# A feed-forward's first product as seven half-size products, on one core

## The chip, the core and the metric

The kernel runs on one core of one Trainium2 chip. The metric is the device time of one execution in microseconds. The engines are TensorE (PE in the rows, its weight loads PEld), VectorE (DVE), ScalarE (ACT), GpSimd (POOL), and SyncE (SP), which issues the transfers.

## What is computed

The reference is a transformer block of another kind followed by two layers of a second block, all on 512 tokens of 1024 features. What matters here is the feed-forward, which stands twice in each of the two layers, at the start and at the end:

```python
D_FF = 2816

def swiglu(x, w_in, w_out):
    g, u = jnp.split(x @ w_in, 2, axis=-1)
    return (jax.nn.silu(g) * u) @ w_out

for l in range(DEPTH_2):                                  # two layers
    x = x + 0.5 * swiglu(rms_norm_2(x, ffn1_norm[l]), ffn1_w_in[l], ffn1_w_out[l])
    ...                                                   # mixer, memory attention
    x = x + 0.5 * swiglu(rms_norm_2(x, ffn2_norm[l]), ffn2_w_in[l], ffn2_w_out[l])
    x = rms_norm_2(x, block_norm[l])
```

w_in is 1024 x 5632 (gate g, then up u), w_out is 2816 x 1024. All inputs are float32.

## The kernel before, in words

Activations stand transposed: features on the 128 partitions, the 512 tokens along the row. X(k), k = 0 to 7, are the eight 128 x 512 tiles of the residual stream.

**Three passes.** Every large product is made in a rounded type (float32r). Each operand a is split into its rounded value hi and the rest lo = a - hi, and TensorE adds hi*hi, hi*lo and lo*hi. `split` (line 367) does this for a tile: ScalarE rounds (371), VectorE subtracts (372), or 374 and 375 with a gain. `chunk3` (346) does it for weights: a transfer into a `raw` tile (358), ScalarE rounds into `wh` (361), VectorE subtracts into `wl` (362). `gemm_f` (377) issues the three matmuls for each contraction tile (383 to 385), each with its own load of 128 x 128 weights and 512 moving columns. `gemm_f2` (387) interleaves two such products at the start of a feed-forward, so that the last of the eight X tiles is needed late.

**Feed-forward.** `ffn` (1061) works in two halves of 11 inner features tiles each (a features tile is 128 of the 2816). For each one it brings in the weights of gate and up (128 x 2048 numbers, two transfers), makes gate in one PSUM bank and up in another (2 x 8 x 3 = 48 matmuls), multiplies by the norm's row R, applies Silu, multiplies (1076 to 1079) and splits the result into `hh`, `hl` (1080). After 11 tiles the second product runs: for each of the eight output tiles d, 11 x 3 matmuls, and VectorE adds half the sum to X(d) (1088). `Norm` (461) makes the feed-forward's input: for each k it splits gain * X(k) (eight ScalarE and eight VectorE operations of 512 columns), squares X(k) on ScalarE (483) and adds the squares up on GpSimd (488); the row R from these sums is needed only after the first product.

**Buffers.** Tiles come from pools with a fixed number of buffers: w 4 (each for `wh` and for `wl`, 1088 columns wide), x 4 and h 9 (128 x 4 x 512), b 9, p 5 and pt 4 (128 x 512), raw 2 (128 x 1088). PSUM has 3 banks acc, 2 ss, 3 st. The residual stream holds two of the nine h tiles.

**Order.** Each engine executes its own list strictly in order. The lists are written when the program is built: a planner takes the instructions in the order in which the code emits them, but lets a later one go ahead as soon as its inputs and buffers are ready in the planner's own model of time. So ScalarE rounds the next tile's weights before it finishes this tile.

**What the change touches.** The weights' layout in `prep` (line 208 on), `ffn`, and in `second_block` (1788) the places that make the feed-forward's input with `norm_split`. A new class `Blocks` stands beside `Norm`.

Of the kernel before, what the change touches and what calls it, by code (L numbers as in the profile page):

```python
# [18 lines left out]
L2 = 2  # L19
FF = 2816  # L20
NFF = FF // 128
HFF = NFF // 2
EPS = 1e-6
NEG = -1e30
CH = 2176
# [14 lines left out]
def _chunks(w, width):  # L40
    return np.stack([_ktile(w[:, i:i + width]) for i in range(0, w.shape[1], width)])


class Packer:
    def __init__(self):
        self.parts, self.at, self.n = [], {}, 0
# [82 lines left out]
def prep(I):  # L129
# [75 lines left out]

    for l in range(L2):
        for n in ("ffn1", "ffn2"):
            w = I[f"{n}_w_in_2"][l]
            w = np.concatenate([w[:, :FF].reshape(D, NFF, 128), w[:, FF:].reshape(D, NFF, 128)], axis=2).reshape(D, -1)
            A[f"{n}_a{l}"] = _chunks(w, 256)  # L210
            w = I[f"{n}_w_out_2"][l]
            A[f"{n}_b{l}"] = np.concatenate([_chunks(w[:FF // 2], 128), _chunks(w[FF // 2:], 128)])
        w = I["w_mix_in_2"][l]
        A[f"mixq{l}"] = _ktile(w[:, :256])
        A[f"mixkv{l}"] = _ktile(w[:, 256:384])
        sq = w[:, 416:672].reshape(D, 4, 64)[:, [0, 2, 1, 3]].reshape(D, 256)
        za = np.concatenate([w[:, 384:416], sq, w[:, 672:928]], axis=1)
        A[f"mixA{l}"] = _chunks(za, 272)
        A[f"mixN{l}"] = _chunks(w[:, 928:], 256)
        w = I["mla_w_uq_2"][l]  # L220
        A[f"uq{l}"] = np.stack([_ktile(w[:, :384]), _ktile(w[:, 384:])])
        A[f"ukv{l}"] = I["mla_w_ukv_2"][l].reshape(128, 2, 4, 2, 64).transpose(1, 0, 3, 2, 4).reshape(2, 128, 512)
        w = I["w_mix_out_2"][l]
        A[f"mixo_mla{l}"] = _chunks(w[:512], 256)
        A[f"mixo_swa{l}"] = _chunks(w[512:768], 512)
        A[f"mixo_na{l}"] = _chunks(w[768:], 512)
        A[f"memq{l}"] = _chunks(I["mem_w_q_2"][l], 256)
        A[f"memkv{l}"] = _chunks(I["mem_w_kv_2"][l], 256)
        A[f"memo{l}"] = _ktile(I["mem_w_o_2"][l])
        A[f"nab{l}"] = _bias_na(I["na_rel_bias_2"][l])  # L230
# [7 lines left out]
class Prog:  # L238
# [201 lines left out]
    def row(self, cols, R=None):  # L440
        ps = self.row_ps(cols)
        if R is None:
            R = self.p_r.tile([128, 512], F32, name="R", tag="R")
        self.nc.scalar.activation(R, ps, AF.Copy)
        return R
# [15 lines left out]
class Norm:  # L461
# [38 lines left out]
    def row(self):  # L500
        if self._R is None:
            self._R = self.g.row(self.cols())
        return self._R


def nat(i):
# [553 lines left out]

def ffn(g, name, l, xt, x, row, done=None):

    nc, A = g.nc, g.A
    X = tview(xt)
    wa, wb = A[f"{name}_a{l}"], A[f"{name}_b{l}"]
    for half in range(2):
        hh, hl = [g.h(F32R) for _ in range(3)], [g.h(F32R) for _ in range(3)]
        hv = [(hh[f // 4][:, f % 4], hl[f // 4][:, f % 4]) for f in range(HFF)]
        for f in range(HFF):
            wh, wl = g.chunk3(wa[half * HFF + f], 8)  # L1070
            pg, pu = g.acc(), g.ss()
            g.gemm_f2(pg, pu, wh, wl, 0, x) if half == 0 and f == 0 else (
                g.gemm_f(pg, wh, wl, 0, 128, x), g.gemm_f(pu, wh, wl, 128, 256, x))
            R = row()
            s, t = g.b(), g.b()
            nc.vector.tensor_tensor(s, pg, R, op=OP.mult)  # L1076
            nc.scalar.activation(s, s, AF.Silu)  # L1077
            nc.vector.tensor_tensor(t, pu, R, op=OP.mult)
            nc.vector.tensor_tensor(t, t, s, op=OP.mult)
            g.split(t, *hv[f])  # L1080
            g.tick()
        for d in range(KD):
            wh, wl = g.chunk3(wb[half * KD + d], HFF)
            cuts = (0, 256, T) if done and half and d == KD - 1 else (0, T)
            for c in map(slice, cuts, cuts[1:]):
                ps = g.ss()[:, c]
                g.gemm_f(ps, wh, wl, 0, 128, [(a[:, c], b[:, c]) for a, b in hv])
                nc.vector.scalar_tensor_tensor(X(d)[:, c], ps, 0.5, X(d)[:, c], op0=OP.mult, op1=OP.add)
                if done and half:
                    done(d, c)  # L1090
            g.tick()

# [695 lines left out]
def second_block(g, xt):  # L1788
# [1 line left out]
    X = tview(xt)  # L1790
    g.room(512, raw=2, k=1, p=5, pt=4)
    c2 = g.const("c2", g.at[2], g.p_k)
    norm = g.norm_split(X, g.c("ffn1_norm0"))
    x, row = norm.parts, norm.row
    for l in range(L2):
        ffn(g, "ffn1", l, xt, x, row)
        mem = mixer(g, l, xt, c2)
        memory(g, l, xt, mem)
        norm = g.norm_split(X, g.c(f"ffn2_norm{l}"))
        ffn(g, "ffn2", l, xt, norm.parts, norm.row, None if l + 1 < L2 else last_norm(g, xt, g.c(f"block_norm{l}")))  # L1800
        gb = g.c(f"block_norm{l}")
        if l + 1 < L2:

            gg = g.p_s.tile([128, 8], F32, name="gg", tag="gg", bufs=1)
            nc.vector.tensor_tensor(gg, gb, g.c(f"ffn1_norm{l + 1}"), op=OP.mult)
            norm = g.norm_split(X, gg)
            acc2 = None
            for k in range(KD):
                acc2 = norm.add(acc2, X(k), gb[:, k:k + 1])
            x, state = norm.parts, {}  # L1810

            def row(norm=norm, acc2=acc2, gb=gb, state=state):
                if not state:
# [34 lines left out]
```

## Time and profile before

| | |
|---|---|
| three runs | 2881.5, 2891.65 (median), 2895.55 us |
| the profiled execution | 2895.25 us, its span 2893.5 us |
| TensorE busy | 2827.5 us, 98% of the span |
| VectorE, ScalarE, GpSimd busy | 1458.4, 1162.8, 464.0 us |
| moved by DMA | 239.63 MB, 83 GB/s on the mean |

A profile shows one execution, instruction by instruction. A matmul's duration in it contains its way through the array, so that neighbours overlap; how fast they follow each other is read from their starts. The same holds, by less than 0.1 us, for other engines' operations. Where a row of the timeline has "x2", two neighbours of the same line were merged.

### The profile page before, as it was taken

How to read it: one execution, taken by the hardware profiler on the slowest of the kernel's cores; microseconds unless marked ns; L12 is line 12 of the kernel's file. 1: busy time of each engine (PE TensorE's matmuls, PEld its weight loads, DVE VectorE, ACT ScalarE, POOL GpSimd, SP SyncE). 2: the span in 40 equal slices, each digit the busy share in tenths (PEclk: the TensorE clock that was granted, in tenths of full speed). 3: DMA queues.
4: the chain of work that ended last, by engine and by line, in shares of the span. 5: the costliest groups of instructions: out<-in, count | busy, mean ns of one | idle time of the engine just before them, and what ended most of it. 6: DMA issues, size and time to landing. Idle time of an engine off the chain costs nothing.

```text
span 2893.5 us, 37993 instructions
## 1 busy us (share of the span) xinstructions
PE 2827.5 (98%) x15101; PEld 2399.4 (83%) x15101; DVE 1458.4 (50%) x2338; ACT 1162.8 (40%) x2008; POOL 464.0 (16%) x557
## 2 busy tenths in 40 slices
PE   8999999999999999999999999999999899999998
PEld 6798999888888888778888888888888778888887
DVE  5734455445434444677643444534444676644442
ACT  5323444533322235765432234322335765332232
POOL 4422222002000013512200003000013512200001
PEclk9999999999999999999799999999999999799999
DMA  4111222233323232212133323233232212133322
GB/s 154 52 45 59 74 73 74 73 103 122 99 87 105 86 106 75 68 37 66 38 102 90 107 88 108 88 85 112 84 107 70 63 40 72 31 102 90 107 88 80
DMA packets 78322, 239.63 MB, mean 83 GB/s; under 512 B 8512, under 2 KB 14656, under 8 KB 78016
## 3 DMA queue, kind: packets, MB, share of 16 engines
q1 hardware_dynamic: 78144, 237.20, 26.0%
q8 instruction: 119, 1.95, 0.3%
q14 instruction: 59, 0.48, 0.1%
HBM read 235.06 MB, written 2.10 MB: 82 GB/s over the span
## 4 chain that ended last, share of the span: by engine, by line
PE 91%; DVE 4%; ACT 2%; POOL 1%; issue 1%; DMA 0%; DVEq 0%; SPq 0%; ACTq 0%; POOLq 0%
PE ss L383 12%; PE ss L384 12%; PE ss L385 12%; PE acc L383 8%; PE acc L385 8%; PE acc L384 8%; PE acc L406 4%; PE acc L408 4%; PE acc L407 4%; PE st L413 3%; PE acc L1200 2%; PE ss L1236 2%; DVE b L611 1%; PE acc L396 1%; PE acc L395 1%; PE acc L397 1%
## 5 line engine op out<-in xcount | busy, mean ns | idle before, releaser
L362 DVE TENSOR_TENSOR wl<-raw,wh 128x1024 fp32r<-128x1024 f32 (+3 forms) x447 | 506.9, 1134 | 558.9 <-ACT wh L361 558.0
L361 ACT ACTIVATE wh<-raw 128x1024 fp32r<-128x1024 f32 (+3 forms) x459 | 449.9, 980 | 731.8 <-PE ss L384 533.7
L383 PE MATMUL acc<-x,wh 128*128 128x512 f32 x1048 | 412.7, 394 | 8.4 <-ACT wh L361 8.1
L385 PE MATMUL acc<-x,wl 128*128 128x512 f32 x1048 | 413.4, 394 | 0.1
L384 PE MATMUL acc<-x,wh 128*128 128x512 f32 x1048 | 411.3, 393 | 0.0
L383 PE MATMUL ss<-h,wh 128*128 128x512 f32 (+1 forms) x843 | 328.7, 390 | 0.0
L385 PE MATMUL ss<-h,wl 128*128 128x512 f32 (+1 forms) x843 | 326.1, 388 | 0.0
L384 PE MATMUL ss<-h,wh 128*128 128x512 f32 (+1 forms) x843 | 326.0, 388 | 0.0
L488 POOL TENSOR_TENSOR b<-b 128x512 f32<-128x512 f32 (+1 forms) x77 | 106.6, 1385 | 1176.6 <-ACT b L483 1068.6
L383 PE MATMUL ss<-x,wh 128*128 128x512 f32 x672 | 261.5, 389 | 0.1
L385 PE MATMUL ss<-x,wl 128*128 128x512 f32 x672 | 261.4, 389 | 0.0
L384 PE MATMUL ss<-x,wh 128*128 128x512 f32 x672 | 261.4, 389 | 0.0
L406 PE MATMUL acc<-wh,x 128*128 128x256 f32 (+1 forms) x880 | 252.8, 288 | 0.0
L407 PE MATMUL acc<-wl,x 128*128 128x256 f32 (+1 forms) x880 | 252.6, 288 | 0.0
L383 PEld LDWEIGHTS acc<-x,wh 128*128 128x128 f32 x1048 | 198.1, 189 | 50.8 <-ACT wh L361 8.5
L385 PEld LDWEIGHTS acc<-x,wl 128*128 128x128 f32 x1048 | 197.9, 189 | 42.6 <-DVE wl L362 1.6
L408 PE MATMUL acc<-wh,x 128*128 128x256 f32 (+1 forms) x816 | 232.1, 286 | 0.0
L384 PEld LDWEIGHTS acc<-x,wh 128*128 128x128 f32 x1048 | 197.9, 189 | 41.1 <-DVE x L375 0.6
L383 PEld LDWEIGHTS ss<-h,wh 128*128 128x128 f32 x843 | 159.3, 189 | 33.1 <-issue 0.6
L385 PEld LDWEIGHTS ss<-h,wl 128*128 128x128 f32 x843 | 159.5, 189 | 32.4
L384 PEld LDWEIGHTS ss<-h,wh 128*128 128x128 f32 x843 | 159.5, 189 | 31.6 <-issue 0.5
L1077 ACT ACTIVATE b<-b 128x512 f32<-128x512 f32 x88 | 55.6, 632 | 310.0 <-DVE b L1076 309.9
(384 smaller groups left out, 4813.6 us busy)
## 6 DMA issues: line engine op xcount, KB each, us to landing
raw<-in_ffn_a SPq DMA_DIRECT2D x176, 512.0 KB, 3.7
raw<-in_ffn_b SPq DMA_DIRECT2D x64, 384.0 KB, 3.1
raw<-in_ffn_b SPq DMA_DIRECT2D x64, 320.0 KB, 2.9
raw<-in_w_swa SPq DMA_DIRECT2D x36, 512.0 KB, 3.9
raw<-in_w_gate SPq DMA_DIRECT2D x16, 512.0 KB, 3.8
raw<-in_w_qkv SPq DMA_DIRECT2D x12, 512.0 KB, 3.9
raw<-in_mixN SPq DMA_DIRECT2D x12, 512.0 KB, 3.8
raw<-in_mixA SPq DMA_DIRECT2D x8, 544.0 KB, 3.7
```

Source lines behind the costliest of these rows:

```text
L361: nc.scalar.activation(h[:, s], r[:, s], AF.Copy)
L362: low.tensor_tensor(l[:, s], r[:, s], h[:, s].bitcast(F32), op=OP.subtract)
L383: mm(ps, a, xh, start=first and k == 0, stop=False)
L384: mm(ps, a, xl, start=False, stop=False)
L385: mm(ps, b, xh, start=False, stop=last and k == n - 1)
L406: mm(ps, a, wh[k][:, c0:c1], start=k == 0, stop=False, **part)
L407: mm(ps, a, wl[k][:, c0:c1], start=False, stop=False, **part)
L408: mm(ps, b, wh[k][:, c0:c1], start=False, stop=k == n - 1, **part)
L413: self.nc.tensor.transpose(ps[:, i * 128:(i + 1) * 128], src(i), self.ident)
L488: (engine or nc.gpsimd).tensor_tensor(acc, acc, sq, op=OP.add)
L1200: nc.tensor.matmul(self.pso[:, c:c + d], PT[:, hs(j * n + k)], self.v(lo + k, hj), start=k == 0, stop=k == n - 1)
L1236: nc.tensor.matmul(v3(s), self.q[h // 4][:96, i, hs(h % 4)], self.k[h // 4][:96, :, hs(h % 4)], start=True, stop=True)
```

## The change

For a features tile the two contraction halves (k 0 to 3, k 4 to 7), the two outputs (gate, up) and the two halves of the tokens (0 to 255, 256 to 511) make a 2 x 2 block product, which is done with seven products in place of eight (Winograd's variant of Strassen's form). `Blocks` makes the seven blocks of the input once per feed-forward, as sums of the two halves, each split into hi and lo; hi and lo of a block stand side by side in one 512-column row. For each features tile GpSimd makes the four sums of weight blocks. Each product has 4 contraction tiles and 3 passes of 256 columns, and its weights (128 x 512) are split one product at a time. The seven results are combined by accumulating in PSUM and by VectorE additions, with ScalarE copies of a bank between two of its products. The inner features are worked off in thirds of 6, 8 and 8 tiles in place of halves of 11. The next tile's first product is issued in the middle of this tile; loads come one tile ahead, into p tiles for even tiles and into raw tiles for odd ones.

```diff
-HFF = NFF // 2
+THIRDS = ((0, 6), (6, 14), (14, 22))
...
+class Blocks:
+    NAMES = ("11", "T1", "T3", "T2", "21", "22", "T4")
+    def __init__(self, g, xt, gain):
+        nc = g.nc
+        self.g, self.acc, self.n = g, None, T
+        self._rc = self._R = None
+        self.b = {n: g.x4() if i < 4 else g.h(F32R) for i, n in enumerate(self.NAMES)}
+        xs = {}
+        t1, t2 = slice(0, 256), slice(256, 512)
+        def put(name, j, src):
+            t = self.b[name]
+            g.split(src, t[:, j, t1], t[:, j, t2])
+        def diff(a, b):
+            d = g.b()[:, t1]
+            nc.vector.tensor_tensor(d, a, b, op=OP.subtract)
+            return d
+        T1 = g.h()
+        for k in range(KD):
+            x, j = g.b(), k % 4
+            nc.scalar.activation(x, xt(k), AF.Copy, scale=gain[:, k:k + 1])
+            if k < 4:
+                put("11", j, x[:, t1])
+                nc.vector.tensor_tensor(T1[:, j, t1], x[:, t2], x[:, t1], op=OP.subtract)
+                put("T1", j, T1[:, j, t1])
+                nc.gpsimd.tensor_copy(T1[:, j, t2], x[:, t2])
+            else:
+                put("21", j, x[:, t1])
+                put("22", j, x[:, t2])
+                d2 = diff(x[:, t2], T1[:, j, t1])
+                put("T2", j, d2)
+                put("T3", j, diff(x[:, t2], T1[:, j, t2]))
+                put("T4", j, diff(x[:, t1], d2))
+            self.acc = self.add(self.acc, xt(k), None)
+    add, cols, row = Norm.add, Norm.cols, Norm.row
...
 def ffn(g, name, l, xt, x, row, done=None):
...
+    def load(f):
+        if f % 2 == 0:
+            r = [g.p() for i in range(4)]
+        else:
+            r = [t[:, o:o + 512] for t in [g.p_raw.tile([128, CH // 2], F32, name="raw", tag="raw") for i in range(2)] for o in (0, 512)]
+        for i, t in enumerate(r):
+            nc.sync.dma_start(t, wa[f][:, i * 512:i * 512 + 512])
+        a11, a21, a12, a22 = r
+        S1, S2, S4 = (g.b() for i in range(3))
+        for d, a, b, op in ((S1, a21, a22, OP.add), (S2, S1, a11, OP.subtract), (a21, a11, a21, OP.subtract), (S4, a12, S2, OP.subtract)):
+            nc.gpsimd.tensor_tensor(d, a, b, op=op)
+        src[f] = dict(P1=a11, P2=a12, P3=S4, P4=a22, P5=S1, P6=S2, P7=a21)
+    def product(f, n, bank, first, xb):
+        if not slots:
+            h = g.p_w.tile([128, CH // 2], F32R, name="wh", tag="wh")
+            w = g.p_w.tile([128, CH // 2], F32R, name="wl", tag="wl")
+            slots.extend((h[:, o:o + 512], w[:, o:o + 512]) for o in (0, 512))
+        wh, wl = slots.pop(0)
+        g.split(src[f][n], wh, wl)
+        mm = nc.tensor.matmul
+        xt_ = x[xb]
+        for k in range(4):
+            a, b = wh[:, hs(k)], wl[:, hs(k)]
+            mm(bank, a, xt_[:, k, t1], start=first and k == 0, stop=False, skip_group_check=True)
+            mm(bank, a, xt_[:, k, t2], start=False, stop=False, skip_group_check=True)
+            mm(bank, b, xt_[:, k, t1], start=False, stop=k == 3, skip_group_check=True)
+    def keep(bank):
+        t = g.pt()[:, t1]
+        nc.scalar.activation(t, bank, AF.Copy)
+        return t
+    def begin(f):
+        ps[f] = g.acc()[:, t1]
+        product(f, "P1", ps[f], True, "11")
+        ps[f, "p1"] = keep(ps[f])
+    def tile(f, nxt, dst):
+        U, V, W = ps.pop(f), g.ss()[:, t1], g.st()[:, t1]
+        product(f, "P2", V, True, "21")
+        R = row()
+        s, t = g.b(), g.b()
+        nc.vector.tensor_tensor(s[:, t1], V, ps.pop((f, "p1")), op=OP.add)
+        nc.vector.tensor_tensor(s[:, t1], s[:, t1], R[:, t1], op=OP.mult)
+        product(f, "P6", U, False, "T2")
+        u2 = keep(U)
+        product(f, "P7", W, True, "T3")
+        product(f, "P5", U, False, "T1")
+        u4 = keep(U)
+        nc.vector.tensor_tensor(t[:, t2], W, u4, op=OP.add)
+        if nxt is not None:
+            begin(nxt)
+        product(f, "P3", U, False, "22")
+        nc.vector.tensor_tensor(s[:, t2], U, R[:, t2], op=OP.mult)
+        nc.scalar.activation(s, s, AF.Silu)
+        nc.gpsimd.tensor_tensor(s, s, R, op=OP.mult)
+        product(f, "P4", W, False, "T4")
+        nc.vector.tensor_tensor(t[:, t1], W, u2, op=OP.add)
+        nc.vector.tensor_tensor(t, t, s, op=OP.mult)
+        g.split(t, *dst)
+        src.pop(f)
+    load(0)
+    load(1)
+    begin(0)
+    for third, (f0, f1) in enumerate(THIRDS):
+        hh, hl = [g.h(F32R) for _ in range(2)], [g.h(F32R) for _ in range(2)]
+        hv = [(hh[f // 4][:, f % 4], hl[f // 4][:, f % 4]) for f in range(f1 - f0)]
+        for f in range(f0, f1):
+            if 1 < f + 1 < NFF:
+                load(f + 1)
+            tile(f, f + 1 if f + 1 < NFF else None, hv[f - f0])
             g.tick()
         for d in range(KD):
-            wh, wl = g.chunk3(wb[half * KD + d], HFF)
+            wh, wl = g.chunk3(A[f"{name}_b{l}{third}"][d], f1 - f0)
...
-    norm = g.norm_split(X, g.c("ffn1_norm0"))
-    x, row = norm.parts, norm.row
+    norm = Blocks(g, X, g.c("ffn1_norm0"))
+    x, row = norm.b, norm.row
```

The other places in `second_block` that made a feed-forward's input change in the same way, and `prep` stores the first product's weights by features tile in the order of the four blocks, and the second product's by thirds.

## Rows read from the trace of the kernel before

**Rows 1.** The page, parts 1 and 4: engines' busy time; the chain that ended last.
```profile
PE 2827.5 (98%) x15101; PEld 2399.4 (83%) x15101; DVE 1458.4 (50%) x2338; ACT 1162.8 (40%) x2008; POOL 464.0 (16%) x557
...
PE 91%; DVE 4%; ACT 2%; POOL 1%; issue 1%; DMA 0%; DVEq 0%; SPq 0%; ACTq 0%; POOLq 0%
```
**Rows 2.** Busy time by stretch, the first feed-forward: A:B, us long, engines (instructions).
```profile
735.00:1073.00 338.00, 338.00 (x1493) 279.85 (x1492) 148.71 (x182) 105.30 (x132) 8.25 (x6) 1.00 0.31 97
```
**Rows 3.** Timeline of PE, one features tile: start, duration, engine, line, operation, tiles.
```profile
1899.90 0.39 PE L383 MATMUL ss<-x,wh 128*128 128x512 f32 x1
...
1910.78 0.39 PE L383 MATMUL ss<-x,wh 128*128 128x512 f32 x1
```
**Rows 4.** Timeline of PE and of its weight loads, matmuls of 256 columns.
```profile
400.96 0.28 PE L406 MATMUL acc<-wh,x 128*128 128x256 f32 x1
...
403.84 0.28 PE L406 MATMUL acc<-wh,x 128*128 128x256 f32 x1
...
401.20 0.19 PEld L406 LDWEIGHTS acc<-wh,x 128*128 128x128 f32 x1
```
**Rows 5.** Timeline of DVE in a feed-forward; groups by line (count, busy us, mean ns).
```profile
743.31 0.68 DVE L1079 TENSOR_TENSOR b<-b 128x512 f32<-128x512 f32 x1
743.91 1.22 DVE L362 TENSOR_TENSOR wl<-raw,wh 128x1024 fp32r<-128x1024 f32 x1
...
L371 ACT ACTIVATE h<-b 128x512 fp32r<-128x512 f32 x88 | 55.7, 633 | 58.3 <-DVE b L1079 58.0
L1185 ACT ACTIVATE pt<-st 128x256 f32<-128x256 f32 x32 | 11.5, 382 | 14.9 <-PE st L413 14.9
```
**Rows 6.** Timeline of DVE and POOL where the second feed-forward's input is made.
```profile
1426.95 0.75 DVE L375 SCALAR_TENSOR_TENSOR x<-h,cst,x 128x512 fp32r<-128x512 f32 x1
1427.61 0.86 DVE L1735 TENSOR_TENSOR h<-h,acc 128x256 f32<-128x256 f32 x2
1428.39 1.84 DVE L375 SCALAR_TENSOR_TENSOR x<-h,cst,x 128x512 fp32r<-128x512 f32 x1
1430.16 0.41 DVE L1735 TENSOR_TENSOR h<-h,acc 128x256 f32<-128x256 f32 x1
1430.49 1.46 DVE L375 SCALAR_TENSOR_TENSOR x<-h,cst,x 128x512 fp32r<-128x512 f32 x1
...
1436.98 2.31 DVE L362 TENSOR_TENSOR wl<-raw,wh 128x1024 fp32r<-128x1024 f32 x1
1439.22 1.77 DVE L375 SCALAR_TENSOR_TENSOR x<-h,cst,x 128x512 fp32r<-128x512 f32 x1
1440.91 1.21 DVE L362 TENSOR_TENSOR wl<-raw,wh 128x1024 fp32r<-128x1024 f32 x1
...
1428.38 12.05 POOL L488 TENSOR_TENSOR b<-b 128x512 f32<-128x512 f32 x7 [40.50 <-issue]
```
**Rows 7.** Timeline of POOL and DVE where the other engine is not at work.
```profile
682.33 1.29 POOL L488 TENSOR_TENSOR b<-b 128x512 f32<-128x512 f32 x1 [8.94 <-ACT b L483]
...
715.08 0.74 DVE L375 SCALAR_TENSOR_TENSOR x<-h,cst,x 128x512 fp32r<-128x512 f32 x1
715.74 0.74 DVE L375 SCALAR_TENSOR_TENSOR x<-h,cst,x 128x512 fp32r<-128x512 f32 x1
```
**Rows 8.** Timeline of ACT and PE at that feed-forward's start: first, last and before it.
```profile
1425.87 0.72 ACT L374 ACTIVATE x<-h,cst 128x512 fp32r<-128x512 f32 x1 [1.87 <-DVE h L1735]
...
1436.34 0.62 ACT L483 ACTIVATE b<-h 128x512 f32<-128x512 f32 x1
...
1430.82 0.28 PE L385 MATMUL acc<-h,wl 128*128 128x256 f32 x1
```
**Rows 9.** Timeline of DVE: the last X before the first feed-forward of either layer.
```profile
712.75 1.28 DVE L1057 TENSOR_TENSOR h<-h,acc 128x512 f32<-128x512 f32 x2
...
1791.64 0.69 DVE L1088 SCALAR_TENSOR_TENSOR h<-ss,h 128x512 f32<-128x512 f32 x1 [1.26 <-PE ss L385]
```
**Rows 10.** The page, part 6: transfers of the first product's weights, KB each, us to landing.
```profile
raw<-in_ffn_a SPq DMA_DIRECT2D x176, 512.0 KB, 3.7
```

More of the change, by code (lines that the diff above doesn't have):

```diff
@@ L207, in prep @@
         for n in ("ffn1", "ffn2"):
-            w = I[f"{n}_w_in_2"][l]
-            w = np.concatenate([w[:, :FF].reshape(D, NFF, 128), w[:, FF:].reshape(D, NFF, 128)], axis=2).reshape(D, -1)
-            A[f"{n}_a{l}"] = _chunks(w, 256)
+            w = I[f"{n}_w_in_2"][l].reshape(2, 4, 128, 2, NFF, 128).transpose(4, 2, 0, 3, 1, 5)
+            A[f"{n}_a{l}"] = w.reshape(NFF, 128, 2048)
             w = I[f"{n}_w_out_2"][l]
-            A[f"{n}_b{l}"] = np.concatenate([_chunks(w[:FF // 2], 128), _chunks(w[FF // 2:], 128)])
+            for j, (a, b) in enumerate(THIRDS):
+                A[f"{n}_b{l}{j}"] = _chunks(w[a * 128:b * 128], 128)
         w = I["w_mix_in_2"][l]
@@ L1064, in ffn @@
     X = tview(xt)
[L1065 to L1080, printed above, removed]
+    wa = A[f"{name}_a{l}"]
@@ new lines, in ffn @@
+    t1, t2 = slice(0, 256), slice(256, 512)
+    src, slots, ps = {}, [], {}
+    def load(f):
[10 more added lines that the diff above has]
+        src[f] = dict(P1=a11, P2=a12, P3=S4, P4=a22, P5=S1, P6=S2, P7=a21)
@@ L1084, in ffn @@
-            cuts = (0, 256, T) if done and half and d == KD - 1 else (0, T)
+            wh, wl = g.chunk3(A[f"{name}_b{l}{third}"][d], f1 - f0)
+            last = done and third == 2
+            cuts = (0, 256, T) if last and d == KD - 1 else (0, T)
             for c in map(slice, cuts, cuts[1:]):
[L1086 to L1089, printed above, removed]
+                pd = g.ss()[:, c]
+                g.gemm_f(pd, wh, wl, 0, 128, [(a[:, c], b[:, c]) for a, b in hv])
+                nc.vector.scalar_tensor_tensor(X(d)[:, c], pd, 0.5, X(d)[:, c], op0=OP.mult, op1=OP.add)
+                if last:
@@ L1798, in second_block @@
         memory(g, l, xt, mem)
-        norm = g.norm_split(X, g.c(f"ffn2_norm{l}"))
-        ffn(g, "ffn2", l, xt, norm.parts, norm.row, None if l + 1 < L2 else last_norm(g, xt, g.c(f"block_norm{l}")))
+        norm = Blocks(g, X, g.c(f"ffn2_norm{l}"))
+        ffn(g, "ffn2", l, xt, norm.b, norm.row, None if l + 1 < L2 else last_norm(g, xt, g.c(f"block_norm{l}")))
         gb = g.c(f"block_norm{l}")
@@ L1805, in second_block @@
             nc.vector.tensor_tensor(gg, gb, g.c(f"ffn1_norm{l + 1}"), op=OP.mult)
-            norm = g.norm_split(X, gg)
+            norm = Blocks(g, X, gg)
             acc2 = None
@@ L1809, in second_block @@
                 acc2 = norm.add(acc2, X(k), gb[:, k:k + 1])
-            x, state = norm.parts, {}
+            x, state = norm.b, {}
             def row(norm=norm, acc2=acc2, gb=gb, state=state):
```

## The prediction

> **What bounds the kernel now.** The page's first part comes first: TensorE is busy 98% of the span, VectorE 50%, GpSimd 16%, and the chain that ended last runs through TensorE for 91% [rows 1]. Next, the stretch view of a feed-forward: in 338 us TensorE never rests and starts 1493 matmuls, 0.226 us each, while GpSimd works 8 us [rows 2]. So time there is matmuls times their spacing, and everything else hides. The timeline gives the spacing: 48 matmuls of 512 columns, one tile of the first product, start over 1899.90 to 1910.78: 10.88 us, 0.2267 each [rows 3]. (The 0.39 us beside each row is latency; only starts count.) Matmuls of 256 columns, which the change uses, run in the first block: 24 starts from 400.96 to 403.84, so 0.120 us each, though each loads its own weights for 0.19 us, so that these loads overlap [rows 4].
>
> **TensorE's own gain.** A tile of 128 features (there are 4 x 22 = 88) takes 7 products x 4 contraction tiles x 3 passes = 84 matmuls x 0.120 = 10.08 us in place of 10.88. Gain 0.80 us a tile, 70.4 us in all: not the eighth that the product count promises, since a narrow matmul costs more than half a wide one. The second product keeps its 528 wide matmuls per feed-forward. The Trainium skill (TensorE: Matmul & The Clock Gate, section Back-to-back issue gap) gives a lone spacing as columns over 2.4 GHz plus about 2.5 ns; worked out from that, an estimate is 48 x 0.216 - 84 x 0.109 = 1.2 us a tile, some 105 us in all, and the sum below would be 35 us lower. The rows stand 11 ns above that for either width, and they decide.
>
> **What the other engines now do per tile.** Before, VectorE and ScalarE were half idle. After, per tile:
> VectorE: seven low halves of weights, the product t*s and t's low half, nine 512-wide operations at 0.60 us start to start; five 256-wide ones at 0.33 [rows 5, 6]. That is 5.40 + 1.65 = 7.05 us of 10.08, if nobody disturbs it.
> ScalarE: seven roundings, Silu and t's rounding at 0.63, three copies out of PSUM at 0.38: 6.8 us [rows 5]. It hides.
> GpSimd: four sums of weights and s*R, each 1.29 us when alone [rows 7]: 6.5 us. It would hide too, but for VectorE.
>
> **GpSimd in VectorE's way.** The start of the second feed-forward is the one stretch where both work hard. Alone, a 512-wide VectorE operation there takes 0.74 us, 0.66 start to start [rows 7]. While GpSimd's seven sums run, it takes 1.46 to 1.84, and the 1024-wide one 2.31 in place of 1.22 [rows 5, 6]. The 256-wide additions L1735, which read one operand from PSUM, stay at 0.41 amid the same sums. So operations with both operands in SBUF wait for GpSimd, those with one in PSUM don't. From 1428.39 to 1440.91 VectorE did six of 0.66, one of 1.14 (1.22 less the 0.08 by which neighbours overlap) and three of 0.33: 6.1 us of work in 12.5, so that each of the seven sums cost it 0.92 us.
> A new tile has nine and a half such SBUF operations beside five of GpSimd. VectorE's cost is then 7.05 + 5 x 0.92 = 11.65 us, more than TensorE's 10.08 and the old 10.88. Bounds per GpSimd operation: 0 (it falls wholly into VectorE's rests) and 1.29 (VectorE waits for all of it); I take 0.92, the row whose mix of operations is nearest.
> The Trainium skill (SBUF — State Buffer, section Who interferes with whom) says that of two such operations the second is blocked until the first ends. The direction agrees with the rows; the size is less here, since operations with a PSUM operand get through.
>
> **What the slow tiles cost.** The excess shows only in runs of tiles: in a third's second product (8 features x 8 x 3 x 0.2267 = 43.5 us) TensorE needs little of VectorE, which gets ahead. How far is set by buffers: six weight slots beside the last chunk (3.6 us) and the four sums of one load (3.7 us); and the last tile's closing operations (1.5 us) lie under the second product. For 8 tiles: 93.2 - 8.8 = 84.4 against TensorE's 80.6, excess 3.8. The first third, 6 tiles, starts straight after the norm with three split products ahead: 69.9 - 1.8 - 3.7 - 1.5 = 62.9 against 60.5, excess 2.4. Per feed-forward 3.8 + 3.8 + 2.4 = 10.0, four times: 40 us. With 0 per GpSimd operation it is 0; with 1.29 (13.5 a tile) it is 17.1 + 17.1 + 12 = 46.2, four times 185.
>
> **The starts.** Before, TensorE runs into each feed-forward without a rest. Now Blocks gives VectorE 44 operations of 256 columns (3 for each of four k, 8 for each of the others) where the norm had 8, and ScalarE 28 roundings beside its 16 operations. P2 needs row block 21 of the last k, P6 and P7 sums from it.
> Second feed-forward of a layer: X is final only between 1425.87 and about 1433 [rows 6, 8]. VectorE from 1426.95: 44 x 0.33 = 14.5, six additions to X 2.0, seven sums of squares 6.4, four half-wide GpSimd copies about 1.8 by the same rate: 24.7, to 1451.7; block 21 of the last k seven operations earlier, 1449.4. TensorE's work before ends at 1431.1 [rows 8], P1 covers 1.4: idle 17. By ScalarE alone (19.8 us: 9.2 as now plus 28 x 0.38) it would be 11 to 12. I take 15, range 10 to 20, twice: 30.
> First feed-forward, layer 0: the last two X tiles land at 714.0 [rows 9]; 16 x 0.33 + 3 x 0.92, less the last seven: P2 at 719.8, TensorE idle from 712.8 but for P1: 5.6. Layer 1: one X tile late, at 1792.3 [rows 9]: about 2; there Blocks wants a tenth of nine h tiles, which waits for the old ones (up to 6 more). Sum 38, range 25 to 56.
>
> **Parts at nothing.** Copies of U between its products: ScalarE 0.38, behind one rounding 1.01; TensorE does another product meanwhile, 1.44 us. P4 waits for VectorE's t = W + copy, with P1 and P3 between (2.9 us). If a copy is late, all matmuls queued behind wait. Second product behind the last tile: the closing chain 0.33 + 0.60 + 0.63 + 0.60 + two GpSimd waits of 0.92 is 4.0 us; the other seven features cover 4.8, five cover 3.4 (before: ten, 6.8), so up to 0.6 once per feed-forward. SP issues four loads per tile for two; a load lands in about 3.7 us [rows 10] and has a tile's time. Third sums: 8 more additions to X per feed-forward, read from PSUM, in the idle stretch.
>
> **Sum** against the profiled execution, 2895.25 us (span 2893.5, 1.75 around it): -70.4 + 40 + 38 = +7.6, so 2902.9. That execution stands 3.6 above the median of the runs, so 2899.3: I say 2900. About 0.5% (14.5 us) is what a measurement of this kernel can tell from no change.
>
> **Rivals.**
> A, the forecast: VectorE held by GpSimd sets the tile's pace (11.4 to 12.0 us a tile, 21 to 68 us of excess, starts 30 to 40), 2871 to 2930. For it: rows 6. Chance 0.42.
> B: the two engines mesh. GpSimd works when VectorE waits or reads PSUM, the sums run in the second product, TensorE sets the pace: -70.4 + 0 + 30, so 2851 by the median. For it: a feed-forward's second products last 22 x 24 x 0.2267 = 120 us, in which GpSimd has nothing of its own to do; the per-tile work of either alone fits. Against: two tiles' buffers don't let sums go far ahead. 0.30.
> C, slower: the waits are longer and come on operations that hide nothing. Place: the runs of 8 tiles. Price by the worst of [rows 6], 2.31 - 1.22 = 1.09 per GpSimd operation: tile 12.5, excess 9.9 + 9.9 + 6.8 = 26.6 per feed-forward, 106 in all, starts 45: +81, so 2973. Gain and losses cancel at a tile of 11.55 us; from there each 0.1 us costs 7.8 in all. 0.19.
> D: VectorE waits for the whole of every GpSimd operation: -70.4 + 185 + 50, so 3056. 0.06. That would be the rule of the Trainium skill on blocking (SBUF — State Buffer, section Who interferes with whom) at its strictest.
> E, the gain isn't there: narrow matmuls with new weights each time run at the load's 0.19 us, 16.0 us a tile: +447, about 3340. Against: rows 4 show just this form at 0.120. 0.03.
> Faster by over 0.5% (under about 2877): most of B (0.27) and A's lower edge (0.04), 0.31. Within: 0.22 of A, 0.03 of B, 0.25. Slower: 0.16 of A, C, D, E, 0.44. The range, 2845 to 2985, holds A, nearly all of B and half of C. A's own is 2871 to 2930.
>
> **What would show it.** Matmuls of the first product 0.120 apart inside a product: the gain. GpSimd's 512-wide sums at 1.6 to 2.5 us, VectorE's 512-wide low halves at 1.2 to 1.8, VectorE busy near 100% in tiles of 11 to 12 us, TensorE waiting there for VectorE's wl: A or C. Tiles of 10.1 us with no wait: B. TensorE's longest rests at the two second feed-forwards' starts, 10 to 20 us, ended by VectorE or ScalarE. I am wrong if TensorE waits in the tiles for ScalarE or for loads, if tiles are even over a third, or if the starts cost nothing.

## The result and the profile after

| | before | after |
|---|---|---|
| median of the runs (four of either kernel) | 2889.73 us | 3118.03 us |
| lowest, highest | 2881.5, 2895.55 | 3110.38, 3123.47 |
| the profiled execution, its span | 2895.25, 2893.5 | 3123.47, 3121.6 |

The ratio is 1.079, 95% interval 1.0754 to 1.0826: 228 us slower, where 10 were forecast, and above the range of 2845 to 2985 us. The page of the changed kernel, parts 1 and 4, answers to [rows 1]:

```profile
PE 2850.6 (91%) x18260; PEld 2535.6 (81%) x18260; DVE 2053.3 (66%) x3186; ACT 1424.3 (46%) x2792; POOL 1168.2 (37%) x1013
...
PE 69%; DVE 19%; issue 6%; ACT 5%; POOL 1%; DMA 1%; DVEq 0%; SPq 0%; ACTq 0%; POOLq 0%
DVE wl L373 9%; PE ss L384 6%; PE ss L385 6%; PE ss L386 6%; PE acc L407 4%; PE acc L409 4%; PE acc L408 4%; PE acc L1145 3%; PE acc L1143 3%; PE acc L1144 3%; PE acc L384 3%; PE acc L385 3%; PE acc L386 3%; PE st L414 2%; DVE b L1163 2%
```

TensorE now rests 9% of the span, and a fifth of the chain lies on VectorE, half of that on the weights' low halves (wl, L373). The waits of the changed kernel (engine, tile and line waiting, releaser: us in total, times, longest) name the same pair:

```profile
POOL b L1129 <- DMA raw<-in_ffn_a: 336.5, 38, 27.2
...
ACT wh L372 <- PE acc L1144: 99.8, 58, 3.4
...
DVE b L1173 <- PE acc L1145: 65.6, 48, 3.0
...
PE ss L1145 <- DVE wl L373: 50.2, 60, 3.7
...
DVE b L1177 <- PE st L1145: 45.1, 47, 1.5
PE st L1145 <- DVE wl L373: 43.7, 27, 1.9
```

TensorE waits for low halves of weights, and VectorE waits for products (L1173, L1177). Neither of the two is the bound throughout. GpSimd's sums (L1129) wait most, for loads.

**Where the 228 us are.** A feed-forward is taken from the end of the VectorE addition that completes its X to the end of the one that completes the next. Before, the four last 360.5, 358.3, 364.1 and 363.5 us, after 416.8, 417.1, 418.1 and 421.4: 227.0 of the 228.1 by which the spans differ. Mixers and the first block are unchanged. TensorE's own work in one, 22 tiles and the second product's 528 matmuls, is 22 x 10.08 + 528 x 0.2267 = 341.5 us (before 359.1). So the four hold 307 us in which it rests or runs slowly, before 10.

**One pair of tiles.** The busy view of the changed kernel in two neighbouring stretches of the first feed-forward (A:B, us long, busy us and instructions of PE, PEld, DVE, ACT, POOL, granted clock, DMA share, GB/s):

```profile
879.18:891.24 12.06, 10.51 (x85) 9.98 (x83) 8.99 (x17) 5.70 (x11) 1.30 (x2) 1.00 0.39 120
891.24:905.85 14.61, 11.06 (x86) 10.45 (x86) 14.55 (x14) 6.28 (x14) 14.42 (x9) 1.00 0.21 67
```

and VectorE's and GpSimd's timelines inside the second (start, us, engine, line, operation, tiles):

```profile
896.42 1.52 DVE L1163 TENSOR_TENSOR b<-b,R 128x256 f32<-128x256 f32 x1
897.87 1.77 DVE L373 TENSOR_TENSOR wl<-raw,wh 128x512 fp32r<-128x512 f32 x1
899.56 1.77 DVE L373 TENSOR_TENSOR wl<-b,wh 128x512 fp32r<-128x512 f32 x1
901.26 0.41 DVE L1177 TENSOR_TENSOR b<-st,pt 128x256 f32<-128x256 f32 x1
```
```profile
897.62 1.47 POOL L1175 TENSOR_TENSOR b<-b,R 128x512 f32<-128x512 f32 x1
899.05 1.74 POOL L1129 TENSOR_TENSOR b<-p 128x512 f32<-128x512 f32 x1
900.86 1.59 POOL L1129 TENSOR_TENSOR b<-b,p 128x512 f32<-128x512 f32 x1
```

GpSimd makes eight sums and one s * R without a pause. In the lines above, VectorE's operations with two SBUF operands last 1.5 to 1.8 us, one for one with GpSimd's, while L1177, with an operand in PSUM, stays at 0.41. Of line 1163 (two SBUF operands), 34 rows lie wholly beside GpSimd's work: 31 of them last 1507 to 1524 ns and three 1066 to 1072, and the 47 beside none last 410 to 426. All rows of L1162, L1169, L1173 and L1177 (one operand in PSUM) last 406 to 425. This is what the Trainium skill states (SBUF — State Buffer, section Who interferes with whom): a VectorE instruction contends with a GpSimd instruction that reads SBUF if it has two SBUF inputs, and not if it has at most one and is outside VectorE's two-port modes. The trace agrees.
The slow stretch has 86 matmuls, 10.3 us of TensorE's work at 0.120 each, in 14.6 us. The quiet one has 85, 10.2 in 12.1, and VectorE is idle there for 3.1.

### The profile page after: what moved, and what is told of

It is laid out like the page before. It is cut to its first block, busy times and chain, and to the rows that moved or that the text cites. A ratio compares the mean times of both kernels' runs of the same rounds, so it can differ in the third digit from the quotient of the medians.

```text
span 3121.6 us, 47277 instructions
## 1 busy us (share of the span) xinstructions
PE 2850.6 (91%) x18260; PEld 2535.6 (81%) x18260; DVE 2053.3 (66%) x3186; ACT 1424.3 (46%) x2792; POOL 1168.2 (37%) x1013
## 4 chain that ended last, share of the span: by engine, by line
PE 69%; DVE 19%; issue 6%; ACT 5%; POOL 1%; DMA 1%; DVEq 0%; SPq 0%; ACTq 0%; POOLq 0%
DVE wl L373 9%; PE ss L384 6%; PE ss L385 6%; PE ss L386 6%; PE acc L407 4%; PE acc L409 4%; PE acc L408 4%; PE acc L1145 3%; PE acc L1143 3%; PE acc L1144 3%; PE acc L384 3%; PE acc L385 3%; PE acc L386 3%; PE st L414 2%; DVE b L1163 2%
## 5 line engine op out<-in xcount | busy, mean ns | idle before, releaser
L362 ACT ACTIVATE wh<-raw 128x1024 fp32r<-128x1024 f32 (+3 forms) x251 | 255.1, 1022 | 343.0 <-PE ss L385 116.7
L363 DVE TENSOR_TENSOR wl<-raw,wh 128x1024 fp32r<-128x1024 f32 (+3 forms) x239 | 281.7, 1185 | 180.7 <-ACT wh L362 180.1
L1145 PE MATMUL acc<-x,wl 128*128 128x256 f32 x1056 | 301.8, 292 | 38.9 <-DVE wl L373 38.5
L373 DVE TENSOR_TENSOR wl<-b,wh 128x512 fp32r<-128x512 f32 x264 | 293.6, 1114 | 56.5 <-ACT wh L372 56.0
L1143 PE MATMUL acc<-x,wh 128*128 128x256 f32 x1056 | 309.2, 293 | 12.9 <-ACT wh L372 11.4
L1144 PE MATMUL acc<-x,wh 128*128 128x256 f32 x1056 | 304.1, 289 | 8.3 <-DVE x L373 8.3
L1175 POOL TENSOR_TENSOR b<-b,R 128x512 f32<-128x512 f32 x88 | 129.8, 1475 | 412.9 <-ACT b L1174 412.9
L372 ACT ACTIVATE wh<-b 128x512 fp32r<-128x512 f32 x264 | 164.2, 624 | 237.2 <-PE acc L1144 85.4
L421 POOL TENSOR_TENSOR s<-s,half 128x4 f32<-128x4 f32 (+4 forms) x97 | 108.6, 1125 | 353.2 <-DVE s L420 341.8
L373 DVE TENSOR_TENSOR wl<-raw,wh 128x512 fp32r<-128x512 f32 x176 | 232.4, 1321 | 9.6 <-ACT wh L372 9.3
L384 PEld LDWEIGHTS ss<-h,wh 128*128 128x128 f32 x840 | 158.2, 189 | 55.8 <-ACT wh L362 13.6
L1129 POOL TENSOR_TENSOR b<-raw 128x512 f32<-128x512 f32 x44 | 61.5, 1397 | 339.2 <-DMA raw<-in_ffn_a 336.5
```

The source lines that it names most:

```text
L362: nc.scalar.activation(h[:, s], r[:, s], AF.Copy)
L363: low.tensor_tensor(l[:, s], r[:, s], h[:, s].bitcast(F32), op=OP.subtract)
L373: nc.vector.tensor_tensor(lo, src, hi.bitcast(F32), op=OP.subtract)
L384: mm(ps, a, xh, start=first and k == 0, stop=False)
L1143: mm(bank, a, xt_[:, k, t1], start=first and k == 0, stop=False, skip_group_check=True)
L1144: mm(bank, a, xt_[:, k, t2], start=False, stop=False, skip_group_check=True)
```

## The experiments

In all diffs the lines are of the changed kernel unless said otherwise. Each time is a median; ratios are to the kernel before on the same chip, with a 95% interval. The part of a profiled execution outside the four feed-forwards took 1435 to 1453 us from run to run, with no tie to the edit. Differences of some 15 us are therefore read from the feed-forwards' own sums (one execution each) and not from the medians.

**1. The sums on VectorE.**
```diff
-            nc.gpsimd.tensor_tensor(d, a, b, op=op)
+            nc.vector.tensor_tensor(d, a, b, op=op)
```


> The four weight sums of a tile go from GpSimd to VectorE; nothing else changes. Theory 1 (VectorE's operations on two SBUF operands alternate one for one with GpSimd's, and that slows the weight splits for which TensorE waits): VectorE has 7.05 + 4 x 0.60 = 9.45 us a tile and one GpSimd operation left to wait for, about 10.4 us a tile, so of the 57 us that a feed-forward's tiles lose now some 45 come back; 2900 to 2960 us. Theory 2 (the loads come late, because an odd tile's two raw buffers are given back late; who makes the sums is no matter): VectorE now waits for the load itself, with everything behind it; 3050 us or more.

2934.0 us, ratio 1.0153 (1.0067 to 1.0238). Theory 1, as forecast: 184 of the 228 us are back, although VectorE does 2.4 us more per tile by itself. Four tiles of this kernel, in the view by stretch:

```profile
857.18:898.50 41.32, 41.32 (x345) 41.23 (x344) 41.32 (x75) 23.97 (x48) 11.10 (x4) 1.00 0.34 104
```

Both engines are busy all the time, 10.3 us a tile: 7.05 + 2.4 + 0.92 for s * R is 10.37, the prediction's own prices. TensorE loses nothing beside a full VectorE: 345 matmuls at 0.120 are 41.4 us. Seven tiles in a row take 70.7 to 70.9 us in the second and last third of all four feed-forwards, where TensorE's own work is 70.6.

**2. No sums at all.** The products read loaded blocks (P3 a12, P5 a21, P6 a11); the sums are left out.

> The weight sums are left out: the products take plain weight blocks (a11, a21, a12) in place of S1, S2, S4 and the fourth sum. All loads, splits, matmuls and buffers stay. Theories 1 and 2 both: TensorE sets the tile's pace, 10.1 us a tile; what remains over TensorE's own work is the starts, 15 to 20 us each; 2860 to 2900 us. A third theory (the split of weights one product at a time, or the copies of a bank between its products, costs TensorE waits by itself): tiles of 11 us or more, over 2950 us.

2942.9 us, 1.0183 (1.0098 to 1.0269). Neither: what is left, some 53 us over the kernel before despite TensorE's 70 us gain, isn't the sums. It isn't VectorE's work either. Seven tiles take 73.7 or 76.3 us, more than with the sums on VectorE, though VectorE is busy for only 30.0 of 41.7 us in four tiles. The chain in 861 to 903 us holds no VectorE at all, but TensorE and ScalarE's roundings (wh), and these wait for products. The busy view of the four tiles, and this wait in 860 to 902:

```profile
859.60:901.30 41.70, 40.32 (x326) 39.20 (x325) 30.00 (x56) 22.70 (x47) 4.90 (x4) 1.00 0.33 102
```
```profile
ACT wh L372 <- PE acc L1141: 7.1, 4, 2.3
```

Number 18 comes back to this.

**3. Finer load buffers.** Four `raw` buffers of half the width in place of two, each load with its own.

> The same SBUF, but raw is four buffers of half the width in place of two, so that each of an odd tile's four blocks gives its buffer back by itself; every other user of raw loads in two pieces. Sums stay on GpSimd. Theory 2 or a mix of it with 1 (loads of odd tiles late, GpSimd idle before them and then eight sums in one run, VectorE at half pace during the run): the sums spread out, a pair of tiles falls from 26.1 us to 23 or 24, 2980 to 3040 us. Theory 1 alone (VectorE is full at 13 us a tile in whatever order the sums come): 3100 to 3130 us.

3125.9 us, 1.0817 (1.0718 to 1.0916). No change, as theory 1 alone has it. But GpSimd's 336 us of waiting for loads are still 301 here, so the edit hardly did what it was made for. That the loads aren't needed for the loss is shown by 13, where none of the first product's loads is waited for.

**4. The thirds alone**, in the kernel before.
```diff
-    for half in range(2):
+    for third, (f0, f1) in enumerate(THIRDS):
```


> The kernel before with one part of the change: the inner features in thirds of 6, 8 and 8 tiles. All theories: 8 more VectorE additions a feed-forward, hidden, and a shorter cover for the last tile of a third; 2885 to 2900 us. If thirds cost by themselves (TensorE waits at the third boundary of each feed-forward): 2900 to 2930 us.

2888.9 us, 1.0004 (0.9974 to 1.0034). Thirds cost nothing here.

**5. Sums made, not used.** The third sum goes into S1's buffer as well, so that a21 stays as loaded.
```diff
-        src[f] = dict(P1=a11, P2=a12, P3=S4, P4=a22, P5=S1, P6=S2, P7=a21)
+        src[f] = dict(P1=a11, P2=a12, P3=a12, P4=a22, P5=a21, P6=a11, P7=a21)
```


> The change, but the products read the loaded weight blocks themselves, as in the run without sums (2942.9 us), while GpSimd still makes four sums per tile, into buffers that nobody reads (the output differs). Theory 'contention': GpSimd's operations slow VectorE wherever they run, used or not; VectorE's work per tile is again 7.05 + 5 x 0.92 = 11.65 us, and the time goes back up to 3020 to 3120 us. Theory 'lateness': what costs is that products wait for sums that come late, not VectorE's pace; then the time stays near the run without sums, 2940 to 2980 us, though VectorE's 512-column operations still take 1.7 us beside a sum.

3197.0 us, 1.1075 (1.1025 to 1.1125): above even "contention". The theory that products wait for late sums falls. GpSimd's work, used by nobody, costs 254 us here.

**6, 7, 8. The starts.** In 6 to 8 the sums are on VectorE. 6: `R = row()` and its first use stand behind P3, the tile's sixth product. 7: also `put("22", ...)` and `put("T4", ...)` two steps later. 8: also `load(0)` and `begin(0)` in `Blocks`, ahead of k = 4.

> The sums on VectorE (2934.0 us by itself), and the norm's row R, with the multiplication of gate's first half by it, moved from behind the tile's second product to behind its sixth. In the trace of the run with sums on VectorE, TensorE's list holds the row's eight matmuls early in the first tile, and they wait for a GpSimd operation of 6.2 us (TensorE rests 729 to 732.9). Theory: that rest, 3.5 to 5.5 us at each of four starts, goes: 2910 to 2925 us. Rival: VectorE's work left over from the blocks is the end of that wait anyway, and the time stays at 2929 to 2939 us.

2918.0 us, 1.0113 (1.0067 to 1.0158). Inside the theory's range, but by luck, as the feed-forwards below show.

> As the run before this one, and in the making of the blocks the two that are used last (22 and T4) come two steps later, behind the blocks 21, T2 and T3 that the first products read. Theory 'order': TensorE rests at the starts because VectorE makes late blocks before early ones; 3 to 6 us less at each start, so 12 to 24 us below the run before this one. Rival 'amount': VectorE has some 12 us of work left when the last X tile is there, and TensorE waits for its end in any order: within 5 us of the run before this one.

2928.1 us, 1.0132 (1.0094 to 1.0171).

> As the run before this one, and the first tile's load, its four sums and its first product (which reads only blocks of the first four X tiles) are issued in the middle of the making of the blocks, in place of behind it. Theory: the sums and splits of the first tile's weights then stand ahead of the blocks of the last X tiles on VectorE, and some 5 us of the 12 us left over go; TensorE rests 5 us less at each start: 15 to 30 us below the run before this one, near or below the kernel before (2890 us). Rival: the blocks of the last tiles are then later by as much: within 8 us of it.

2922.8 us, 1.0125 (1.0096 to 1.0155). The row's wait that number 6 aims at stands in the timeline of experiment 1 (in brackets the idle time before, and what ended it):

```profile
732.90 2.07 PE L437 MATMUL ss<-cst,rc 128*128 128x128 f32 x8 [3.54 <-POOL rc L421]
```

It went, but the starts didn't shorten. From the completed X to the closing multiplication (t * s) of the third tile the four took 57.6, 64.2, 59.4 and 64.4 us in experiment 1 and 55.3, 67.2, 60.8 and 63.5 in 6; the sums of the four feed-forwards are 1479.7 and 1478.7, and the 15 us between the spans lie in the mixers, which the edit doesn't touch. So 6's theory falls, and 7's and 8's fall with it (1484.8 and 1482.8): neither row nor order is the limit.

**9. The sums spread out.** One sum behind each of P6, P7, the next tile's P1 and s * R; `sums` issues the next of the list.
```diff
-        for d, a, b, op in ((S1, a21, a22, OP.add), (S2, S1, a11, OP.subtract), (a21, a11, a21, OP.subtract), (S4, a12, S2, OP.subtract)):
-            nc.gpsimd.tensor_tensor(d, a, b, op=op)
+        todo.extend(((S1, a21, a22, OP.add), (S2, S1, a11, OP.subtract), (a21, a11, a21, OP.subtract), (S4, a12, S2, OP.subtract)))
...
+        sums(1)
```


> The change, with the same four sums per tile on GpSimd, but each issued behind another product of the tile (behind the sixth, the seventh, the next tile's first, and the fourth behind s * R), in place of all four ahead of the tile. In the trace of the change GpSimd makes eight sums and one s * R in one run of 14.6 us in every second tile, in which VectorE is at half its pace. Theory 'run': what costs is that run, because VectorE can get ahead by at most the eight product buffers; spread out, VectorE's average (11.65 us per tile) sets the pace in place of 13.0, and the time falls by some 88 x 1.35 = 119 us, to 2980 to 3050 us. Rival 'count': the number of GpSimd operations sets the cost wherever they stand: 3100 to 3135 us.

3113.5 us, 1.0798 (1.0724 to 1.0872): the range of "count". But the trace shows that the sums were hardly spread, since those of an odd tile still begin when its load lands (GpSimd's timeline):

```profile
884.53 1.30 POOL L1135 TENSOR_TENSOR b<-raw 128x512 f32<-128x512 f32 x1 [3.52 <-DMA raw<-in_ffn_a]
...
890.61 1.61 POOL L1183 TENSOR_TENSOR b<-b,R 128x512 f32<-128x512 f32 x1 [1.37 <-ACT b L1182]
...
896.30 1.61 POOL L1135 TENSOR_TENSOR b<-b,p 128x512 f32<-128x512 f32 x1 [0.68 <-POOL b L1135]
897.87 1.74 POOL L1135 TENSOR_TENSOR p<-p 128x512 f32<-128x512 f32 x1
```

Eight of GpSimd's operations stand in these 15.1 us, with 2.1 us of pauses. So this run doesn't decide between "run" and "count". That a run of eight isn't needed for the loss is shown by 13 (five in a row) and 14 (three).

**10. Half the sums.**
```diff
-            nc.gpsimd.tensor_tensor(d, a, b, op=op)
+            (nc.vector if f % 2 else nc.gpsimd).tensor_tensor(d, a, b, op=op)
```


> The change with the sums of the odd tiles on VectorE, so that GpSimd makes four sums and two s * R per two tiles. Theory 'amount': VectorE's work is 2 x 7.05 + 4 x 0.6 + 6 x 0.92 = 22.0 us per two tiles, 11.0 per tile against 10.1 with all sums on VectorE: 2934 + 88 x 0.9 = 3013, 2995 to 3040 us. Theory 'run': no run of eight sums is left, VectorE's lead covers four sums, and the tiles go back to 10.1 to 10.5 us: 2935 to 2975 us.

3071.8 us, 1.0658 (1.0583 to 1.0732). Above both. Half the sums keep 138 of the 184 us, with VectorE busy 45.0 of 50.3 us in four tiles:

```profile
873.56:923.82 50.26, 43.61 (x339) 42.20 (x338) 45.01 (x66) 23.79 (x48) 18.27 (x12) 0.97 0.28 85
```

So VectorE's mean doesn't set the time.

**11, 12. Squares on TensorE**: four one-column matmuls per X tile in place of GpSimd's additions, on 6 and on 8. The sums of squares, and so R, aren't the reference's in this form.

> As the run with the row later and all sums on VectorE (2918.0 us), and the sums of the norm's squares are added up by TensorE (four matmuls of one column per X tile, into one PSUM bank), in place of GpSimd's 8 additions at a start (16 at the third feed-forward, 12.2 us of GpSimd in one run there). Theory 'amount and port': VectorE's work left over at a start is slowed by these additions, up to 0.9 us for each that meets it; 3 to 8 us less at each start, 2888 to 2906 us. Rival: the small matmuls stand in TensorE's list and wait for ScalarE's squares, which gives as much back: 2912 to 2930 us.

2929.5 us, 1.0167 (1.0096 to 1.0237): the rival's range.

> As the run before this one, with the order of the run in which the first tile's load, sums and first product stand in the middle of the blocks (2922.8 us). Theory: the two add up, since with GpSimd out of the way the early sums run while VectorE has time: 2875 to 2898 us, within 0.5% of the kernel before or under it. Rival: the buffers that the early sums hold keep the blocks of the fifth and sixth X tile back, as in that run: within 8 us of the run before this one.

2920.2 us, 1.011 (1.0027 to 1.0193): neither. In 12 three starts shorten, to 54.1, 50.8 and 54.5, and the third lengthens to 71.0, because there TensorE works through the small matmuls of two rows, 64 in one run (its timeline in 12):

```profile
1821.67 11.55 PE L569 MATMUL st<-cst,b 128*128 128x1 f32 x64
```

**13, 14. GpSimd work without weights**, on experiment 2 (sums left out); 14 has `range(2)`.
```diff
+        z = g.b()
+        for i in range(4):
+            nc.gpsimd.tensor_tensor(z, z if i else R, R, op=OP.mult)
```


> The run without sums (2942.9 us), with four GpSimd multiplications per tile that read only the norm's row R and a buffer of their own, issued behind s * R: GpSimd is as busy as in the change, but waits for no load and keeps no weight buffer (the sums are left out, the output differs). Theory 'port': what costs is VectorE at half its pace beside GpSimd, and its lead of eight product buffers doesn't make that good: as the change or slower, 3090 to 3200 us. Theory 'average': the port costs only what brings VectorE over TensorE, 7.05 + 5 x 0.92 = 11.65 against 10.5 us per tile: 3020 to 3060 us, VectorE fully busy. Theory 'loop': in the change the sums delay the release of load buffers, and so the next loads; without that the port hurts little: 2943 to 2990 us.

3178.9 us, 1.0999 (1.096 to 1.1039): "port". Four GpSimd operations per tile that touch no load and no weight cost 236 us. "Loop" and "average" fall. Four tiles of it, and two of its waits (its line 1170 is the change's 1173, its 1142 the change's 1145):

```profile
878.86:930.71 51.85, 41.84 (x312) 39.38 (x311) 42.42 (x55) 22.35 (x46) 26.85 (x19) 0.97 0.26 78
```
```profile
DVE b L1170 <- PE acc L1142: 120.6, 76, 6.1
...
PE st L1142 <- DVE wl L373: 55.8, 51, 1.7
```

A tile lasts 13.0 us, with VectorE idle for 2.4 of it and TensorE not busy for 2.5: each waits for the other in turn.

> As the run before this one with two such multiplications in place of four. VectorE's work is 7.05 + 3 x 0.92 = 9.8 us per tile, under TensorE's 10.1. Theory 'port' (a run of slowed work isn't made good): about half of what four cost, 3010 to 3080 us. Theories 'average' and 'loop': no more than without them, 2935 to 2965 us.

2997.8 us, 1.0366 (1.0331 to 1.0402), between the two ranges. Two cost 55 us, four 236: a quarter, not half, but not nothing, although 7.05 + 3 x 0.92 = 9.8 is under TensorE's 10.08. Four tiles:

```profile
861.03:903.41 42.38, 39.84 (x312) 37.81 (x311) 34.41 (x55) 22.26 (x46) 14.11 (x11) 1.00 0.30 94
```

One rival to the port would be that the planner wrote other lists when GpSimd got more to do. The traces exclude it: by lines and tile names, VectorE, ScalarE and TensorE execute the same operations in the same order in 14 as in 2. In 13 only six or seven of VectorE's operations, two of ScalarE's and a handful of TensorE's stand a few places elsewhere in each feed-forward. What differs is GpSimd's work and the time that VectorE's operations take beside it. The chain shows where that falls: VectorE isn't on it in four tiles of 2, and in 14 its low halves (L373, wl) hold 12% of it and the closing t * s (L1178) 6%, in 13 20% and 9%.

**15. No differences in Blocks.**
```diff
-                put("T3", j, diff(x[:, t2], T1[:, j, t2]))
+                put("T3", j, x[:, t2])
```
and likewise T2 and T4.

> As the run with the row later and all sums on VectorE (2918.0 us), with the blocks T2, T3 and T4 split from the scaled X itself: 12 of the blocks' 44 VectorE operations per start, 4.5 us at 0.375, are left out (the output differs). Theory 'amount': TensorE waits at a start for VectorE's work left over, and each microsecond less of it is worth one or more, since TensorE runs at half its clock behind the rest: 4 to 8 us per start, 2886 to 2902 us. Rival: what is waited for at the starts is ScalarE, buffers or loads: 2908 to 2924 us.

2907.3 us, 1.0061 (1.0039 to 1.0082). 10.7 us less by the medians, between the two. The feed-forwards' sums fall by 16.7 (1478.6 to 1461.9): 12 VectorE operations of 4.5 us in all are worth some 4 us per start. So VectorE's amount counts there, nearly one for one, at the lower edge of "amount".

**16. The version that the runs then pointed to.**

> All sums on VectorE, the row later, the first tile's load, sums and first product amid the blocks; the squares of the first, second and fourth feed-forward added up by TensorE into 32 columns of a PSUM bank (VectorE adds the eight of each), those of the third, which needs two rows, on GpSimd as in the change but each beside its own X tile and not all at the end. In the run with both rows' squares on TensorE the first, second and fourth start took 54.1, 50.8 and 54.5 us against 55.3, 67.2 and 63.5 with the row later alone, and the third 71.0 against 60.8. Theory: the third goes back to 60 and the others stay: 2920 - 11 = 2909, 2895 to 2915 us, still slower than the kernel before. Rival: it gets under 2890 us, if the third gains as the others do.

2914.3 us, 1.0091 (1.0058 to 1.0124), as forecast. The starts sum to 217 us against 247 in 6, but the next three tiles of the second and fourth feed-forward give 15 of the 30 back. It is still slower than the kernel before.

**17, 18. Half the lead**, on 13 and on 2.
```diff
-            slots.extend((h[:, o:o + 512], w[:, o:o + 512]) for o in (0, 512))
+            slots.append((h[:, :512], w[:, :512]))
```


> The run with four GpSimd multiplications per tile that touch no weights (3178.9 us), with one product's weights in each of the four weight buffers in place of two, so that VectorE can be at most four products ahead of TensorE in place of eight. Theory 'lead': a tile costs more than either engine's mean because VectorE, slowed for some 8 us and free for some 5, can't work ahead far enough; with half the lead more of the slowed stretch falls on TensorE: 3210 to 3330 us. Rival: the lead has no part in it: 3160 to 3200 us.

3140.6 us, 1.0921 (1.0848 to 1.0994).

> The same halving of the buffers in the run without sums and without those multiplications (2942.9 us). There VectorE has 3 us to spare in each tile and is slowed by s * R alone, so both theories expect little: 2940 to 2975 us. A larger rise would say that four buffers are too few by themselves, and the run beside this one would tell nothing.

2896.6 us, 1.0044 (1.0011 to 1.0078). Both are below all that was expected. By the medians they are 38 and 46 us faster than 13 and 2, by the feed-forwards' sums 33 and 37, so the theory of the short lead falls; the price of the four operations, 244 us between these two, is that of the longer lead (236). In 18 seven tiles take 71.5 to 72.7 us, so most of what number 2 lost in its tiles is gone. A reason that fits the waits in 2 is that a buffer with two products' weights comes free only when both are used. It isn't shown alone, since the planner wrote other lists for 17 and 18. Single buffers together with real sums on VectorE weren't tried.

## Why the prediction was wrong

The account from the feed-forwards' sums: -70.4 from TensorE's work, +103.7 for what remains with the sums on VectorE (1479.7 less 4 x 341.5 is 113.7, before 10.0), +193.7 for the sums on GpSimd (1673.4 - 1479.7); together 227.0. Forecast: -70.4, +38, +40. The 103.7 lie at the starts, since the later tiles of experiment 1 take no longer than TensorE's own work. Of the 193.7, some 24 lie there as well: up to the third tile's t * s the four feed-forwards take 270 us in the change and 246 in experiment 1.

**TensorE's gain: right.** Of 7392 matmuls of the first product 6717 follow their neighbour by 0.10 to 0.14 us.

**VectorE's price: right.** 7.05 + 5 x 0.92 = 11.65 us per tile makes 46.6 in four; a stretch of four tiles in the second third of the changed kernel shows 46.68 busy, in 54.37 us:

```profile
879.18:933.55 54.37, 44.37 (x338) 42.37 (x336) 46.68 (x57) 23.98 (x48) 31.45 (x20) 0.97 0.27 78
```

**"What the slow tiles cost": wrong, and this is the step that failed.** It took the tile's time as VectorE's work, 11.65 us, and credited 8.8 us per run of eight tiles for VectorE getting ahead. A tile took 12.2 to 13.3 us (85.2 to 93.0 over seven). Eight tiles, with TensorE's time in the second product taken off, took 95 to 105 us where the sum had 84.4, so the credit was not there either. Tiles even over a third were one of the prediction's own signs of being wrong. Charged 40 us, it cost 194, some 170 of them behind the starts. Experiments 13 and 14 show in its place that GpSimd at work beside VectorE makes the tile longer than either engine's own work, even at 9.8 us of VectorE's work. A full VectorE alone doesn't do that: in experiment 1 both engines are busy all the time and nothing is lost. Why VectorE's idle time couldn't be used is not settled. Loads that come late (13), lateness of the sums (5), other lists (14) and a short lead (17) are excluded as its cause, and a run of eight isn't needed (13, 14). The clock is a part: in the change some 400 of the first product's matmuls run at the lower clock, about 40 us over 0.120 each, in experiment 1 140, about 14 us. What is left for the rest is the fixed order of the lists, in which a slowed operation holds back those behind it: in 13 VectorE stands 121 us before L1170 waiting for a product, and TensorE behind for a low half that comes later in VectorE's list. That is argued from the waits and wasn't tried.

**The starts: right in place, too small by more than half.** Charged 38 us, they cost about 104 with the sums on VectorE. The first feed-forwards of the two layers, charged 5.6 and 2, lost 21 and 20; the second ones, charged 15 each, 31 and 32. Nor was it one rest of 10 to 20 us: TensorE's longest at a start of the changed kernel is 6.3. The bounds given with the 38, 25 and 56, don't follow from its terms, which give 28 and 54; nothing hangs on that. The busy view of the changed kernel at the first start:

```profile
714.00:720.00 6.00, 1.69 (x8) 0.88 (x6) 6.00 (x14) 4.39 (x13) 2.52 (x2) 0.98 0.00 0
720.00:726.00 6.00, 1.67 (x8) 1.67 (x9) 6.00 (x7) 3.93 (x8) 5.23 (x5) 0.50 0.00 0
726.00:732.00 6.00, 3.54 (x16) 3.46 (x17) 6.00 (x10) 1.23 (x3) 2.82 (x3) 0.50 0.14 44
```

The prediction had TensorE idle for 5.6 us here, until block 21 is made. But VectorE is busy without a pause for 18 us: GpSimd's sums, of squares and of weights, slow the blocks' operations, and behind the blocks stand the low halves of the next products. VectorE's timeline, four operations beside no GpSimd and three beside it:

```profile
714.54 1.42 DVE L373 TENSOR_TENSOR x<-b,x 128x256 fp32r<-128x256 f32 x4
...
721.38 4.31 DVE L373 TENSOR_TENSOR h<-b,h 128x256 fp32r<-128x256 f32 x3
```

TensorE has some 30 matmuls in 18 us, where it could start 150, two thirds of the stretch at the lower of its two clocks (0.50), which follows its rest.

**Parts at nothing: right** for the thirds (4). Late loads aren't needed for the loss (13); what GpSimd's waiting for them costs in the change itself was not measured, since 3 left the waits in place. **The rivals:** D's total, 3056, came nearest, but not by its mechanism, since VectorE's share per GpSimd operation was the 0.92 of A. B's condition, that the engines mesh, failed: idle time was there on both sides and didn't meet.

## What to carry to other kernels

When two engines hand work back and forth inside one tile, don't take the larger of the two averages as the tile's time once a third engine slows one of them in places: treat the slowing as added in good part to the tile. Being full is not the harm by itself, since in experiment 1 both were full and nothing was lost. Work moved to a helper engine "for nothing" is to be checked for shared ports first: here 2.4 us of sums per tile were cheaper on VectorE, which they filled, than on GpSimd, which had the time. And count a product's saving together with what the making of its operands puts ahead of its first matmul.

## What was not expected of the hardware

After a rest, TensorE was at the lower clock (1.2 GHz, granted 0.50) from 720 to 732; in the changed kernel some 400 of the first product's matmuls stand 0.20 to 0.25 us apart, about 40 us over 0.120. And GpSimd's operations pay as well: its 512-wide sums last 1.40 to 1.71 us on the mean, against 1.29 alone [rows 7].
